# Order of grouped and memory heads, and a planner's constants, in a two-layer hybrid encoder trunk

## Chip, cores and metric

The kernel runs on one core of one Trainium2 chip. The metric is the device time of one execution in microseconds (us), as a median over several runs. Traces are of one profiled execution each, with times counted from the start of its span.

## The reference

Two layers on 1024 tokens of width 1024. Each layer normalises its input, multiplies it with one combined input projection of 3072 columns and feeds three groups of heads in parallel:

- 6 differential heads: two softmaxes each, `softmax(q1 k1) - lam * softmax(q2 k2)`, times `v`, then a per-head norm. q and k of 32 columns are turned by rotary tables.
- 6 grouped-query heads over 2 key/value heads, q and k of 64 columns with a per-head norm and a 2-D rotary.
- 4 cross-attention heads into 256 memory tokens, whose keys and values are projected from `mem`.

Cut to what matters:

```python
proj = rms_norm(x, pre_norm[l]) @ w_in[l]
oa = (softmax(q1 @ k1.T * s1) - lam * softmax(q2 @ k2.T * s1)) @ v     # 6 heads, then a norm
ob = softmax(gq @ gk.T * s2) @ gv                                      # 6 heads, 2 kv heads
om = softmax(mq @ mk.T * s2) @ mv                                      # 4 heads, 256 keys
y = concat(oa * silu(dgate), ob * silu(ggate), om * silu(mgate)) @ w_out[l]
x = x + rms_norm(y, post_norm[l])
```

All of it is float32 to the outside.

## The kernel before

**Precision by parts.** Each float32 factor of a projection is split into a high and a low part; a product is three products (high by high, high by low, low by high). Scores are made in float32 with the parts stacked along the rows of the contraction. The exponentials, 1024 columns per unit, are split into two float16 tiles `eh` (a copy on ScalarE or VectorE, lines 902 and 903) and `el` (the difference, on POOL or VectorE, lines 905 and 904).

**Items.** Attention is cut into items, each of which has three steps. *Load*: `fetch_stream` walks a list of items in order, waits for the item's `needs`, and issues its q (and k) rows from scratch in HBM through SyncE's queue. *Maxima*: `max_stream` walks the same list; TensorE makes scores in 512-column products (line 1071 for differential items, 1283 and 1284 for grouped heads, 1338 and 1339 for memory heads), VectorE takes their row maxima (line 942), and `nm_rows` turns these into two more contraction rows and stores them next to q by DMA (lines 914 to 924). *Units*: `stream` makes the scores again with the maxima subtracted inside the product (lines 1081, 1295 and 1296, 1349 and 1350), ScalarE takes the exponential (line 898), and every second unit (for memory heads every unit) `pv_part` multiplies with the values (lines 531 to 533) and ScalarE stores the result (line 994). There are 12 differential items d0 to d11 of 8 units, 6 grouped items g0 to g5 of 8 units, and 4 memory items m0 to m3 of 2 units. The grouped and memory items make one list, in the order of `GS_ORDER` (line 73). At its end `fin_g` scales a head with its gate on VectorE (lines 1200 to 1204).

**Buffers between items.** A grouped head's q rows lie in `a0`, `b0` or `a1`, `b1`, by its number's parity, so its load waits for `free` of the grouped head two before it. All memory heads have the one pair `ma`, `mb`, so a memory head's load waits for `free` of the memory head before. `free` fires when an item's last unit has been made. These tiles take slots of the ring `big`, which come free as the last projection chunk (`gg0`) finishes its 8 token tiles: `b0` and `mb` come before `b1`.

**Stages of a layer.** First the projections that the first heads need, then the differential items with the other nine projection chunks beside them (line 520), then grouped and memory items, with the splitting of the output weights and the finishing of the heads beside them, then the output projection (line 1448). When the list's last maxima have been issued, the first output tile (`z0`) is begun in the freed single banks of PSUM.

**What sets the order.** Every engine runs its instructions in the order in which they were written. That order comes from `Plan`, a small event model which runs while the kernel is built: each piece of work names an engine, a duration and a priority, and the instruction is written when the model starts it. Its durations are in `PE`, `ACT`, `DVE` and `POOL` (lines 328 to 339), e.g. `DVE_FIX` (line 75) plus columns at 960 per us for VectorE. `LAT` is the delay until another engine may go on. `SLACK` (line 81) is added after transfers. Where a step may run on two engines, the model takes the one with less queued. `DU` (line 69) is the least distance of two units' starts in the model, counted from the first unit of the stream, for differential items and for the grouped and memory list.

**PSUM.** Two tiles of two banks and four of one bank are handed out by `Banks` in the order of priority. `KINDS` (line 83) has for each kind its priority (lower goes first), how many it may hold at once, and its size in banks: `mx` are the products for maxima, `st` the projection chunks beside attention, `tr` transposes, `pv` products with the values, `zh` the first output tile. All of these are single banks.

```python
        def stream(items, kind, t0, du):
...
                for u in range(it.n_units):
                    yield "until", t_start + nu * du
                    nu += 1
                    slot = yield take_ps("un")
```

Of the kernel before, what the change touches and what calls it, by code (L numbers as in the profile page):

```python
# [65 lines left out]
LO_BIAS = (6, 1)  # L66
NAT, SQ, GS = 3, 1, 1
ALT0, ALT1, ALTM = (), (), ()
DU = (3.0, 0.0)
MXP = (0, -0.5)  # L70
SV_PRIO = -1
UNP, PVP, STP, POST, FIN = 0, 0.2, 0.5, -1, 2
GS_ORDER = ('g0', 'm0', 'g1', 'm1', 'g2', 'm2', 'g3', 'm3', 'g4', 'g5')
LAT = {"pe": 0.231, "act": 0.176, "dve": 0.165, "pool": 0.121, "hwdge": 0.65, "dma": 0.95}
DVE_FIX = 0.15
PV_N = 2
X_GATE, XT, AHEAD = 5, 5, 2
DMA_RATE = 300.0

CLOCK_WINDOW, CLOCK_LOW, CLOCK_HIGH = 3.41, 0.33, 0.85  # L80
SLACK = 0.8

KINDS = {'un': (0.5, 2, 2), 'z': (1, 2, 2), 's0': (2, 2, 1), 's1': (0, 2, 1), 'st': (1, 4, 1), 'pv': (1, 1, 1), 'tr': (-1, 2, 1), 'mx': (2, 4, 1), 'zh': (3, 2, 1)}


def raw(t):
    return t.bitcast(F32)
# [200 lines left out]
def trunk(ctx, tc, t_in, t_out):  # L288
    nc = tc.nc
    act, dve, pool, pe = nc.scalar, nc.vector, nc.gpsimd, nc.tensor  # L290
# [13 lines left out]
    banks = Banks({2: [psp.tile([P, D], F32, name=f"pp{i}") for i in range(2)],  # L304
                   1: [psp.tile([P, 512], F32, name=f"ps{i}") for i in range(4)]}, KINDS)
    R = {"rt": Ring(RT_BUFS), "wt": Ring(W_SLOTS), "big": Ring(16)}
# [9 lines left out]
    def use(eng, dur, fn, prio=0, lat=None, port=False):  # L316
        return "use", eng, dur, fn, prio, lat, port

    def wait(ev):
        return "wait", ev  # L320
# [8 lines left out]
        return use("pe", ncols / 2210.0, fn, prio, lat)  # L329

    def ACT(n, fn, prio=0, src="s"):
        return use("act", (0.2 if src == "s" else 0.17) + n / 1200.0, fn, prio)

    def DVE(n, fn, prio=0, ops=1, fast=False, port=False):

        return use("dve", DVE_FIX * ops + n / (1900.0 if fast else 960.0), fn, prio, None, port)

# [11 lines left out]
    def dmas(lst, prio=0):  # L349
        ev = Event(len(lst))  # L350
        for o, i, kb in lst:
            pl.spawn(dma(o, i, kb, prio), ev)
        return ev
# [43 lines left out]
    def split_w(rt, p2=None, name=None):  # L397
        if p2 == "big":
            wi = yield take("big")
            t = new_big()  # L400
            hi, lo = (t[:, h * 512:(h + 1) * 512].rearrange("p (a n) -> p a n", a=2) for h in range(2))
        elif p2 is None:
            wi = yield take("wt")
            hi = wp.tile([P, 2, NC], F32R, name="wt")
            lo = wp.tile([P, 2, NC], F32R, name="wt")
        else:
            wi = None
            hi = p2.tile([P, 2, NC], F32R, name=name + "h")
            lo = p2.tile([P, 2, NC], F32R, name=name + "l")
        yield ACT(512, lambda: act.activation(hi, rt, AF.Copy))  # L410
        yield either((DVE(512, lambda: dve.tensor_sub(out=lo, in0=rt, in1=raw(hi)), port=True), W_BIAS[0]),
                     (POOL(512, lambda: pool.tensor_sub(out=lo, in0=rt, in1=raw(hi))), W_BIAS[1]))  # L412
        return hi, lo, wi
# [52 lines left out]
    def split_T(src, hi, lo, halves=(0, 1), prio=0):  # L466

        done = Event(len(halves))

        def half(h):  # L470
            slot = yield take_ps("tr")
            ps = slot[3]

            def f():
                for j in range(4):
                    pe.transpose(out=ps[:, j * P:(j + 1) * P], in_=src(4 * h + j), identity=ident)  # L476

            yield PE(1024, f, prio)
            v = ps[:, 0:512].rearrange("p (b t) -> p b t", t=P)
            yield ACT(512, lambda: act.activation(hi[:, 4 * h:4 * h + 4, :], v, AF.Copy), prio, "p")  # L480
            yield DVE(512, lambda: dve.tensor_sub(out=lo[:, 4 * h:4 * h + 4, :], in0=v,
                                                  in1=raw(hi)[:, 4 * h:4 * h + 4, :]), prio)
            free_ps(slot)

        for h in halves:
            pl.spawn(half(h), done)
        yield wait(done)

    def norm_T(xt, gbc, hn, hi, lo, ev=None, alt=False, prev=None):
        ss = small.tile([P, 1], F32, name="ss")  # L490
        yield ACT(1024, lambda: act.activation(hi.rearrange("p a b -> p (a b)"), xt, AF.Square, accum_out=ss))
        box = []
        yield from rstd_of(ss, 1, 1.0 / D, box, -2)
        if ev is not None:
            yield wait(ev)
            gbc = gbc[0]
        if prev is not None:
            yield wait(prev)
        if alt:
            yield ACT(1024, lambda: act.activation(hn, xt, AF.Copy, scale=box[0][:, 0:1]))  # L500
            yield POOL(1024, lambda: pool.tensor_mul(out=hn, in0=hn, in1=gbc))
        else:
            yield DVE(1024, lambda: dve.scalar_tensor_tensor(out=hn, in0=xt, scalar=box[0][:, 0:1], in1=gbc,
                                                             op0=ALU.mult, op1=ALU.mult), port=ev is None)
        yield from split_T(lambda b: hn[:, b * P:(b + 1) * P], hi, lo, prio=0 if ev is None else -2)
# [33 lines left out]
    def make_layer(l):  # L539
# [370 lines left out]
        def nm_rows(mx, n2, scale, dst, ready):  # L910
# [17 lines left out]
            yield wait(dmas([(dst(j).rearrange("p (a b) -> p a b", b=P), raw(x), 4) for j, x in enumerate((nh, nl))]))  # L928
            yield "until", pl.t + SLACK
            ready.fire(pl)  # L930
# [24 lines left out]
        def fetched(it, ev):  # L955
            for key in it.keys:
                yield wait(gm[key + "_ev"])
            yield wait(ev)
            yield "until", pl.t + SLACK
            it.loaded.fire(pl)  # L960
# [37 lines left out]
        def stream(items, kind, t0, du):  # L998

            prev = None  # L1000
            nu = 0
            t_start = None
            for it in items:
                yield wait(it.ready)
                if t_start is None:
                    t_start = pl.t
                pl.spawn(it.fin())
                boxes, evs = [], []
# [4 lines that stand above are left out]
                    ps = slot[3]  # L1013
                    k = yield take("e32")
                    e32 = Q["at"].tile([P, 1024], F32, name="e32", bufs=E32_BUFS)
                    ncols, mm = it.unit_mm(u)
                    yield PE(ncols, lambda: mm(ps), UNP)
                    box, ev = [], Event()
                    pl.spawn(exp_part(ps, slot, it.scale, kind, box, ev, (e32, k)))
                    boxes.append(box)  # L1020
                    evs.append(ev)
                    if len(boxes) == it.per_pv:
                        d = Event()
                        pl.spawn(pv_part(it, u, boxes, evs, prev, d))
                        prev = d
                        boxes, evs = [], []
                it.free.fire(pl)
# [360 lines left out]
        def wo_setup():  # L1388
# [10 lines left out]
            v = yt[:, 0:768].rearrange("p (t c) -> p t c", t=2)  # L1399
            yield "until", pl.t + 4 * SLACK  # L1400
            yield wait(dmas([(v, y_scr[:, 0:2, 0:384], 384)]))
            yield "until", pl.t + 4 * SLACK
            for t in range(2):
# [259 lines left out]
        def main(nxt):  # L1663
# [22 lines left out]
            for i in range(4):  # L1686
                m_it.append(mk_m(i, m_it[i - 1] if i else None))
            gs = [(g_it if c[0] == "g" else m_it)[int(c[1])] for c in GS_ORDER]

# [5 lines left out]
            def d_stream():  # L1695
                yield wait(vfull["dv0"])
                yield from stream(ds, 0, 0, DU[0])
                d_units.fire(pl)
# [33 lines left out]
            def g_stream():  # L1732
                pl.spawn(fetch_stream(gs))
                pl.spawn(g_max())
                yield wait(d_units)
                yield from stream(gs, 1, 0, DU[1])
                for it in gs:
# [161 lines left out]
```

## Time and profile before

| | us |
|---|---|
| median of 3 runs | 1521.71 |
| lowest and highest of them | 1515.41, 1523.19 |
| the profiled execution | 1515.87 |
| its span, first to last instruction | 1514.1 |
| TensorE (PE) busy | 1469.9 |
| VectorE (DVE) busy | 1012.3 |
| POOL busy | 909.2 |
| ScalarE (ACT) busy | 893.3 |

A stretch's busy time of an engine is the union of its instructions in it; matmuls overlap each other, so a busy TensorE is not one at its peak. A wait is put down to what came last. The chain of waits is followed back from the last instruction of the span, at each step to what released it or to the instruction before it on its engine. PEld is the loading of weights, which runs beside PE. Layers are counted from 0.

### The profile page before, as it was taken

Reading aid. Unit: us, or ns where it says so; the run is one execution under the profiler, and the core shown is the slowest. Engines: PE = TensorE matmul, PEld = TensorE weight load, DVE = VectorE, ACT = ScalarE, POOL = GpSimd, SP = SyncE. Lnnn points to the kernel's source line nnn. Section 1 sums busy time; section 2 is a strip of 40 time slices with the busy share of each in tenths; the row PEclk is TensorE's granted clock in tenths of the full one; section 3 lists DMA queues with packets and bytes.
Section 4 is the critical chain, followed back from the end, with each engine's and each line's share of the span. In section 5 each row is a group of like instructions: output and inputs, shape, how many; then the busy total and the mean of one; then the engine's idle time right before and its main releaser. Section 6 shows DMA issues by size and latency. Waiting matters only on the chain.

```text
span 1514.1 us, 39223 instructions
## 1 busy us (share of the span) xinstructions
PE 1469.9 (97%) x15920; PEld 1362.8 (90%) x15920; DVE 1012.3 (67%) x1887; ACT 893.3 (59%) x1429; POOL 909.2 (60%) x653
## 2 busy tenths in 40 slices
PE   8999999999999999999999999999999999999997
PEld 7999989999999988888899989999999998788886
DVE  6738686777773897825466486776777649876233
ACT  5333747776677587663333346677667757686511
POOL 4233848889777586661132358579888757685400
PEclk9999999999999999999999999999999999999999
DMA  6544313233223644116164524223341256322232
GB/s 220 158 121 130 86 59 107 81 109 106 78 65 93 187 120 105 49 50 214 70 213 129 141 70 117 70 63 101 111 113 58 64 136 195 94 68 72 98 136 98
DMA packets 166658, 164.75 MB, mean 109 GB/s; under 512 B 14924, under 2 KB 140588, under 8 KB 166477
## 3 DMA queue, kind: packets, MB, share of 16 engines
q1 hardware_dynamic: 166477, 162.25, 36.7%
q8 instruction: 125, 2.05, 0.5%
q14 instruction: 56, 0.46, 0.1%
HBM read 111.74 MB, written 50.09 MB: 107 GB/s over the span
## 4 chain that ended last, share of the span: by engine, by line
PE 84%; DVE 5%; issue 3%; POOL 3%; DMA 2%; ACT 1%; SPq 1%; POOLq 0%; DVEq 0%; ACTq 0%
PE ps L520 35%; PE pp L1448 10%; PE pp L1081 6%; PE ps L1071 6%; PE ps L531 4%; PE ps L533 4%; PE ps L532 4%; PE ps L1283 3%; PE ps L1284 2%; PE pp L1295 2%; PE pp L1296 2%; POOL el L905 2%; PE ps L476 2%; DVE mx L942 1%; PE ps L707 1%
## 5 line engine op out<-in xcount | busy, mean ns | idle before, releaser
L905 POOL TENSOR_TENSOR el<-e,eh 128x1024 f16<-128x1024 f32 x254 | 562.6, 2229 | 167.3 <-ACT eh L902 160.1
L520 PE MATMUL ps<-wt,big 128*128 128x256 f32 x4608 | 642.1, 286 | 12.6 <-DVE sl L716 3.4
L520 PEld LDWEIGHTS ps<-wt,big 128*128 128x128 f32 x4608 | 605.0, 191 | 32.7 <-DVE sl L716 3.9
L942 DVE TENSOR_REDUCE mx<-ps 128x1 f32<-128x512 f32 (+1 forms) x608 | 404.0, 684 | 118.2 <-PE ps L1071 79.4
L898 ACT ACTIVATE e<-pp 128x1024 f32<-128x1024 f32 x304 | 309.2, 1023 | 99.9 <-PE pp L1081 53.8
L902 ACT ACTIVATE eh<-e 128x1024 f16<-128x1024 f32 x264 | 277.6, 1058 | 2.9
L531 PEld LDWEIGHTS <-eh 128*128 128x128 f16 x2144 | 194.4, 96 | 13.6 <-issue 9.0
L533 PEld LDWEIGHTS <-el 128*128 128x128 f16 x2144 | 196.1, 99 | 4.8 <-POOL el L905 4.2
L412 POOL TENSOR_TENSOR wt<-rt,wt 128x512 fp32r<-128x512 f32 x83 | 123.2, 1496 | 126.0 <-ACT wt L410 112.2
L532 PEld LDWEIGHTS <-eh 128*128 128x128 f16 x2144 | 196.2, 97 | 0.9 <-issue 0.8
L1071 PE MATMUL ps<-sdk,sdq 96*128 96x512 f32 x384 | 158.7, 413 | 0.8 <-DVE gs L736 0.8
L454 POOL TENSOR_SCALAR u<-ss 128x1 f32<-128x1 f32 (+3 forms) x95 | 24.2, 254 | 224.6 <-DVE ss L1589 96.1
L531 PE MATMUL ps<-vd,eh 128*128 128x65 f16 x1536 | 150.5, 193 | 0.0
L532 PE MATMUL ps<-vd,eh 128*128 128x64 f16 x1536 | 149.6, 194 | 0.0
L533 PE MATMUL ps<-vd,el 128*128 128x65 f16 x1536 | 149.1, 192 | 0.0
L1081 PE MATMUL pp<-sdq,sdk 98*128 98x256 f32 x768 | 124.9, 285 | 0.2 <-DMA sdq<-nl 0.2
L1081 PEld LDWEIGHTS pp<-sdq,sdk 98*128 98x128 f32 x768 | 113.1, 189 | 5.7 <-issue 0.6
L994 ACT ACTIVATE o<-ps 128x130 f32<-128x130 f32 (+1 forms) x160 | 46.1, 288 | 92.0 <-PE ps L533 91.4
L1295 PE MATMUL pp<-big 128*128 128x256 f32 x384 | 99.2, 290 | 0.0
L1296 PE MATMUL pp<-big 67*128 67x256 f32 x384 | 97.7, 286 | 1.3 <-DMA big<-nl 1.2
L410 ACT ACTIVATE wt<-rt 128x512 fp32r<-128x512 f32 x124 | 75.1, 630 | 18.8 <-DMA rt<-in_w_in 7.1
L455 POOL TENSOR_TENSOR r<-u,mhalf 128x1 f32<-128x1 f32 (+3 forms) x95 | 80.7, 850 | 7.9
(244 smaller groups left out, 2621.9 us busy)
## 6 DMA issues: line engine op xcount, KB each, us to landing
rt<-in_w_in SPq DMA_DIRECT2D x96, 128.0 KB
rt<-in_w_in SPq DMA_DIRECT2D x44, 256.0 KB
gt<-g_scr SPq DMA_DIRECT2D x32, 256.0 KB
rt<-in_w_out SPq DMA_DIRECT2D x32, 256.0 KB
sdq<-s_dqa SPq DMA_DIRECT2D x48, 128.0 KB
sdk<-s_dka SPq DMA_DIRECT2D x48, 128.0 KB
big<-s_gqa SPq DMA_DIRECT2D x24, 256.0 KB
big<-s_gqb SPq DMA_DIRECT2D x24, 256.0 KB
```

The lines of the kernel that those rows point to most:

```text
L520: pe.matmul(ps, lhsT=x[:, kt, :], rhs=y[:, a, :], start=(kt == 0 and n == 0), stop=(kt == KT - 1 and n == 2))
L531: pe.matmul(o[:, 0:65], lhsT=eh, rhs=v[:, kt, 0:65], start=(kt == 0), stop=False, skip_group_check=True)
L532: pe.matmul(o[:, 0:64], lhsT=eh, rhs=v[:, kt, 66:130], start=False, stop=False, skip_group_check=True)
L533: pe.matmul(o[:, 0:65], lhsT=el, rhs=v[:, kt, 0:65], start=False, stop=(kt == n - 1), skip_group_check=True)
L898: yield ACT(1024, lambda: act.activation(e, ps, AF.Exp, scale=scale), 0, "p")
L902: yield either((ACT(1024, lambda: act.activation(eh, e, AF.Copy)), 0.0), (DVE(1024, lambda: dve.tensor_copy(out=eh, in_=e), 0, fast=True, ...
L905: (POOL(1024, lambda: pool.tensor_sub(out=el, in0=e, in1=eh)), 0.0))
L942: yield DVE(512, lambda: dve.tensor_reduce(out=out_ap, in_=src, axis=AX.X, op=ALU.max), MXP[0])
L1071: yield (512, lambda ps, n=n: pe.matmul(ps, lhsT=q()[0:96, i * P:(i + 1) * P], rhs=k()[0:96, n * 512:(n + 1) * 512], start=True, stop=True ...
L1081: pe.matmul(ps[:, a * 256:(a + 1) * 256], lhsT=k()[0:98, kt * P:(kt + 1) * P], rhs=q()[0:98, j * 256:(j + 1) * 256], start=True, stop=True)
L1295: pe.matmul(o, lhsT=ka()[:, ks], rhs=a()[:, qs], start=True, stop=False)
L1448: pe.matmul(z, lhsT=x[:, k, :], rhs=y, start=(k == KT_ORDER[0] and n == 0), stop=(k == KT_ORDER[-1] and n == 2))
```

## The change

The list of grouped and memory items becomes g0, g1, m0, g2, m1, g3, m2, g4, m3, g5: from g2 on a memory head stands one grouped head later than before. The kind `mx` may hold three single banks instead of four. The model's figures change: `DVE_FIX` from 0.15 to 0.117 us, the fixed part of a ScalarE instruction from 0.2 to 0.201 us with its source in SBUF and from 0.17 to 0.138 us with it in PSUM, `SLACK` from 0.8 to 0.7 us, and the step of differential units from 3.0 to 2.85 us. No instruction's form or size changes; orders, and choices between two engines, can.

```diff
--- before.py
+++ after.py
@@ -66,21 +66,21 @@
 LO_BIAS = (6, 1)
 NAT, SQ, GS = 3, 1, 1
 ALT0, ALT1, ALTM = (), (), ()
-DU = (3.0, 0.0)
+DU = (2.85, 0.0)
 MXP = (0, -0.5)
 SV_PRIO = -1
 UNP, PVP, STP, POST, FIN = 0, 0.2, 0.5, -1, 2
-GS_ORDER = ('g0', 'm0', 'g1', 'm1', 'g2', 'm2', 'g3', 'm3', 'g4', 'g5')
+GS_ORDER = ('g0', 'g1', 'm0', 'g2', 'm1', 'g3', 'm2', 'g4', 'm3', 'g5')
 LAT = {"pe": 0.231, "act": 0.176, "dve": 0.165, "pool": 0.121, "hwdge": 0.65, "dma": 0.95}
-DVE_FIX = 0.15
+DVE_FIX = 0.117
 PV_N = 2
 X_GATE, XT, AHEAD = 5, 5, 2
 DMA_RATE = 300.0
 
 CLOCK_WINDOW, CLOCK_LOW, CLOCK_HIGH = 3.41, 0.33, 0.85
-SLACK = 0.8
-
-KINDS = {'un': (0.5, 2, 2), 'z': (1, 2, 2), 's0': (2, 2, 1), 's1': (0, 2, 1), 'st': (1, 4, 1), 'pv': (1, 1, 1), 'tr': (-1, 2, 1), 'mx': (2, 4, 1), 'zh': (3, 2, 1)}
+SLACK = 0.7
+
+KINDS = {'un': (0.5, 2, 2), 'z': (1, 2, 2), 's0': (2, 2, 1), 's1': (0, 2, 1), 'st': (1, 4, 1), 'pv': (1, 1, 1), 'tr': (-1, 2, 1), 'mx': (2, 3, 1), 'zh': (3, 2, 1)}
 
 
 def raw(t):
@@ -329,7 +329,7 @@
         return use("pe", ncols / 2210.0, fn, prio, lat)
 
     def ACT(n, fn, prio=0, src="s"):
-        return use("act", (0.2 if src == "s" else 0.17) + n / 1200.0, fn, prio)
+        return use("act", (0.201 if src == "s" else 0.138) + n / 1200.0, fn, prio)
 
     def DVE(n, fn, prio=0, ops=1, fast=False, port=False):
```

## Rows read from the trace of the kernel before

**Rows 1.** The page: busy time of each engine, and the chain by engine.

```profile
PE 1469.9 (97%) x15920; PEld 1362.8 (90%) x15920; DVE 1012.3 (67%) x1887; ACT 893.3 (59%) x1429; POOL 909.2 (60%) x653
...
PE 84%; DVE 5%; issue 3%; POOL 3%; DMA 2%; ACT 1%; SPq 1%; POOLq 0%; DVEq 0%; ACTq 0%
```

**Rows 2.** Busy by stretch: length, PE, PEld, DVE, ACT, POOL; clock, DMA share, GB/s.

```profile
142.90:511.00 368.10, 362.34 (x4501) 347.33 (x4501) 258.81 (x540) 248.16 (x391) 280.22 (x198) 1.00 0.34 95
888.20:1257.10 368.90, 363.10 (x4503) 347.90 (x4504) 260.16 (x539) 248.45 (x392) 280.21 (x198) 1.00 0.34 94
533.10:572.80 39.70, 35.04 (x483) 30.84 (x481) 36.02 (x50) 28.20 (x39) 29.38 (x14) 1.00 0.53 129
1278.60:1318.00 39.40, 35.06 (x484) 30.58 (x481) 35.82 (x50) 28.68 (x41) 29.52 (x14) 1.00 0.53 132
572.80:596.70 23.90, 23.29 (x298) 20.41 (x296) 17.45 (x28) 19.86 (x24) 17.97 (x9) 1.00 0.15 44
596.70:631.20 34.50, 34.28 (x434) 28.97 (x431) 30.33 (x44) 22.40 (x30) 21.30 (x10) 1.00 0.33 79
650.70:674.70 24.00, 22.90 (x378) 21.16 (x378) 5.39 (x4) 17.41 (x23) 18.06 (x9) 1.00 0.06 18
```

**Rows 3.** Chain that ended last, transfers in the grouped part: start, us.

```profile
534.03 6.16 DMA big<-s_mqa
564.93 7.02 DMA big<-s_gqa
...
1309.88 7.22 DMA big<-s_gqa
```

**Rows 4.** Busy by stretch, line 1295 alone: PE and PEld of g0, g1.

```profile
511.50:528.00 16.50, 7.58 (x30) 5.58 (x31) 1.00 0.49 151
533.00:556.60 23.60, 7.75 (x31) 5.88 (x31) 1.00 0.43 103
```

**Rows 5.** Busy by stretch, line 1349 alone: PE and PEld of m0, m1, m2.

```profile
528.90:532.40 3.50, 1.40 (x4) 0.76 (x4) 1.00 0.92 298
557.40:561.50 4.10, 1.27 (x4) 0.66 (x4) 1.00 0.23 64
592.30:594.20 1.90, 1.57 (x4) 0.77 (x4) 1.00 0.00 0
```

**Rows 6.** Busy by stretch: maxima of m2 (line 1338); g2, g3, g5 (line 1283).

```profile
566.50:571.00 4.50, 2.21 (x8) 1.52 (x8) 1.00 1.03 215
...
544.80:562.70 17.90, 6.55 (x16) 3.03 (x16) 1.00 0.06 16
571.20:589.90 18.70, 7.03 (x16) 2.99 (x16) 1.00 0.24 72
624.40:638.80 14.40, 7.35 (x17) 2.89 (x16) 1.00 0.16 46
```

**Rows 7.** Timeline of SyncE's queue, 455 to 512 us: start, us.

```profile
496.94 1.73 SPq L346 DMA_DIRECT2D big<-s_gqa  x3
```

**Rows 8.** Busy by stretch, columns as in rows 2.

```profile
568.00:570.00 2.00, 1.25 (x10) 1.25 (x11) 0.58 (x1) 0.00 (x0) 0.00 (x0) 1.00 1.03 228
1316.00:1318.00 2.00, 0.85 (x4) 0.68 (x4) 0.47 (x2) 0.00 (x0) 0.00 (x0) 1.00 0.94 309
1318.00:1320.00 2.00, 2.00 (x10) 1.80 (x9) 1.04 (x3) 0.13 (x1) 0.00 (x0) 0.59 0.03 12
1320.00:1322.00 2.00, 2.00 (x11) 1.88 (x10) 0.80 (x2) 1.96 (x2) 0.00 (x0) 0.56 0.00 0
```

**Rows 9.** Timelines of ScalarE and of VectorE, 545 to 556 us.

```profile
546.89 1.92 ACT L898 ACTIVATE e<-pp 128x1024 f32<-128x1024 f32 x2
...
550.57 4.40 DVE L942 TENSOR_REDUCE mx<-ps 128x1 f32<-128x512 f32 x7
```

**Rows 10.** Busy by stretch, line 1081 alone: differential units, four products each.

```profile
142.80:189.90 47.10, 10.44 (x64) 9.16 (x64) 1.00 0.32 88
212.20:483.50 271.30, 52.03 (x320) 47.26 (x320) 1.00 0.31 88
```

## Prediction

> **What bounds the kernel now.** I read the page's busy line and its chain first [rows 1]: TensorE is busy 97% of the span and carries 84% of the chain that ended last. The change takes no product away, so only two things can move the end: time in which TensorE has nothing to do, and time at the lower clock. Next I read the busy time by stretch [rows 2]. "Idle" below is a stretch's length less TensorE's busy time. In the differential stretch of each layer it is 368.10 - 362.34 = 5.76 us and 368.90 - 363.10 = 5.80 us. In the grouped and memory part of layer 0 it is 39.70 - 35.04 = 4.66 us between the first units of g1 and g2, then 0.61 us to g3's first unit, 0.22 us to g4's, and 1.10 us in g5's stretch, which runs on to the output projection. Layer 1 repeats the large one: 39.40 - 35.06 = 4.34 us. In that stretch VectorE is busy 36.02 of 39.70 us, so it is nearly a second bound there; in the next it has 17.45 of 23.90.
>
> The chain of waits names what ends the large idle time [rows 3]: transfers of 6.16, 7.02 and 7.22 us of q rows for the next heads. Those loads wait in `fetch_stream` for `prev.free`, the end of the units of the memory head before, since all memory heads share `ma` and `mb`. Behind them stand the maxima, in the order of the list: m1's, then g2's.
>
> **The order of heads.** I follow it as one recurrence. Call c the time from the end of a memory head's units to the first unit of the grouped head that is loaded behind the next memory head. The units of g0 run from 511.5 to 528.0 and g1's from 533.0 to 556.6 [rows 4]; m0's end at 532.4, m1's at 561.5, m2's at 594.2 [rows 5]. With the starts in rows 2, c is 572.8 - 532.4 = 40.4, 596.7 - 561.5 = 35.2 and 631.2 - 594.2 = 37.0 us. Its parts: transfers, 7.0 us [rows 3]; a memory head's maxima, 4.5 us; a grouped head's maxima, 14.4 us where little else competes, 17.9 and 18.7 us elsewhere; from there to the first unit 596.7 - 589.9 = 6.8 or 572.8 - 562.7 = 10.1 us [rows 2, 6]. The shortest sum is 7.0 + 4.5 + 14.4 + 6.8 = 32.7 us.
>
> With the new list, g0 does not change. g1's maxima no longer stand behind m0's. They can't start at once either: g1's q rows are issued at 496.94 whatever the order, since its tiles come free only then [rows 7]. A 6 to 7 us transfer has them in by about 503 to 504, some 4 us before they start now, so its units can start at 533.0 - 4 = 529, about where g0's end; I take 528.5. They take 23.6 us as before [rows 4], m0's two units about 4.9 (4.1 of rows 5 and the last product's tail), and m0 ends at 557.0. g2's loads now wait for g0 alone: 528.0 + 7.0 + 17.9 + 10.1 = 563.0. TensorE is without units for 563.0 - 557.0 = 6.0 us where it is now 572.8 - 561.5 = 11.3.
>
> This gain is given back in part, for m1's work is not done by then and moves behind g2. From there the old pattern runs once per pair: g3 starts c after m0's end; m2 ends 21.4 us after g3's first unit (594.2 - 572.8, the same pair of stretches now); g5 starts c after that, its maxima now standing behind m3's loads. g5's first unit is thus at 557.0 + c + 21.4 + c = 578.4 + 2c, against 650.7 now. They are equal at c = 36.15. Of the measured values I take 34.0, between the shortest sum 32.7 and the 35.2 of the middle pair: TensorE was busy through most of that middle stretch [rows 2], and in the new one a memory head's units and maxima more stand elsewhere. Then g5 starts at 646.4, 4.3 us sooner, and its 24.0 us stretch [rows 2] moves with it. The first output tile still begins after g5's maxima, at 646.4 - 6.8 = 639.6 against 638.8 [rows 6], so its cover stays. Ends: c = 32.7 gives -6.9, c = 37.0 gives +1.7, c = 40.4 gives +8.5 us per layer. Two layers: -8.6 us.
>
> **The clock in that gap.** In layer 1 TensorE is busy 0.85 of 2 us at 1316, and the granted clock then is 0.59 and 0.56 of full (1.2 GHz for most of both rows, 2.4 GHz outside); 2.00 x 0.41 + 2.00 x 0.44 = 1.7 us are lost there [rows 8]. In layer 0 the like stretch at 568 has 1.25 of 2 us and keeps 1.00. Only part of it reaches the end: I count 1.0 us gained in layer 1 when the gap halves; ends 0 and 1.7. The Trainium skill (TensorE: Matmul & The Clock Gate, Part 1: The HAM clock gate) says the throttled state is the default and recent activity is what releases it; layer 1 agrees with its 0.59, layer 0 with 1.00 shows that a gap of this size may pass, and by the rule alone every such gap would pay the price.
>
> **Three products for maxima instead of four.** A maximum takes VectorE 4.40 / 7 = 0.63 us back to back [rows 9]. TensorE makes its pair of products in about 0.41 us (6.55 / 16) [rows 6], so three banks, 1.9 us of VectorE's work, cover it: 0. If TensorE is away longer, with two units' products and the second matrix, VectorE runs dry for one bank's worth, 0.63 us; four times per head this adds 2.5 us to c, which is 5.0 us per layer. Below nothing: a bank left to projections can end some of the idle 5.8 us of the differential stretch; that end is counted with the next edit.
>
> **The planner's figures and slack.** They cost no time and change only orders: 0.033 us less per VectorE operation, 0.032 us less per ScalarE read of PSUM, 0.1 us less after a transfer. The plan had 0.15 + 512 / 960 = 0.683 us for a maximum and has 0.650 now, against 0.63; for an exponential 0.17 + 1024 / 1200 = 1.023 and now 0.991, against 1.92 / 2 = 0.96 [rows 9]. So plan and chip come closer without meeting. What mistimed orders can cost is bounded by the idle time of the differential stretches, 5.76 + 5.80 = 11.6 us: all gone, or as much again. I take an eighth, -1.5 us, since part of each error stays and an idle time may move as well as go.
>
> **The step of 2.85 us.** The first 16 units come in 47.1 us, 47.1 / 16 = 2.94 from edge to edge, near the planned 3.0; the other 80 take 271.3 us, 3.39 each [rows 10]. The pace binds only the first two items, which end 15 x 0.15 = 2.25 us sooner. Nothing is won: TensorE has projections to do beside them (362.34 of 368.10 us busy [rows 2]), which must be done before the grouped heads load. I take 0; ends -2.25 us and, if POOL and ScalarE are crowded by it, +2.25 us per layer.
>
> **Sum.** -8.6 - 1.0 - 1.5 = -11.1 us against the profiled execution's 1515.87 us (span 1514.1 and 1.8 around it): 1504.8. The median of the runs shown, 1521.71, stands 5.8 us above that execution, so the forecast as a median is 1510.6, written as 1511.
>
> **Rivals.** *Slower: VectorE late for three banks.* If the pairs keep the 37.0 us of the third one and the smaller limit adds its 2.5, c is 39.5; g5 starts at 578.4 + 79.0 = 657.4, 6.7 us later per layer, 13.4 in all: 1529.3, as a median 1535. It decides from c = 36.15 upward and is measurable from about 38. For it: VectorE's 36.02 of 39.70 us in the first such stretch [rows 2]. Against: it is near 17 of 24 in the next. *No change: the gap only moves.* With c from 36 to 37, what g2 gains the later pairs give back, and the rest is noise: 1515 to 1519, as a median 1521 to 1525. For it: two of three measured values of c lie above 36.15. *The clock falls in each new gap.* The new order waits ahead of g3 and g5 as it did once ahead of g2. With c at 36.15 and both gaps of both layers paying 1.7 us, that is +6.8: 1522.7, median 1528.5. For it layer 1, against it layer 0 [rows 8]. [...] *The change doesn't do what it says:* the limit of 2.85 is such an edit already; for the whole I see no way, since the list sets the streams directly.
>
> **How the numbers follow.** Forecast 0.50, no change 0.25, slower 0.18, clock 0.07. Half a per cent, 7.6 us, is about what a measurement of this kernel can tell from no change; the runs shown already span 7.8. Faster by more than that: most of the forecast's own 0.50, whose median range runs from 1495 (c = 32.7 twice, 13.8; the clock 1.0; nearly all idle of the differential stretches) to 1518, less a tenth that falls short, and a little from the others: 0.47. Slower: most of its rival and a third of the clock's: 0.19. Same: 0.34. The range 1495 to 1530 leaves out the worst of the slower rival and a full sweep of gains.
>
> **What would show it.** Right: g1's units directly after g0's, at about 529 us; m0's between g1 and g2; a first g2 unit at 560 to 565, and g5's first unit before 650; idle under 3 us where it was 4.66; granted clock 1.00 there in layer 1. Wrong: idle of several us ahead of g3 or g5 with the chain naming q rows or maxima; g5's first unit after 652; VectorE waiting for products inside the maxima; more idle than 5.8 us in the differential stretch.

## The result, and the profile after

The changed kernel takes **1530.13 us** (median; 1528.42 to 1531.01) beside 1521.71 us before: a ratio of 1.0063 [1.0038, 1.0087], slower by 0.63%. That is 8.4 us where 11 us less were forecast, and just outside the range. The profiled execution has 1528.42 us with a span of 1526.6, 12.5 us above the span before; 4.1 us of this are the choice of executions, since the one before stands 5.8 us under its median and this one 1.7. (Three kernels below had one disturbed execution of over 2000 us, which is left out; in `all_but_order` and `warm_products` it was the profiled one, so no row of these two is used.)

The page of the changed kernel, its busy line and its chain by engine, answer to [rows 1]:

```profile
PE 1479.1 (97%) x15920; PEld 1369.0 (90%) x15920; DVE 1033.3 (68%) x1892; ACT 893.7 (59%) x1429; POOL 892.3 (58%) x648
...
PE 81%; DMA 6%; DVE 5%; POOL 3%; issue 3%; SPq 1%; ACT 1%; POOLq 0%; DVEq 0%; ACTq 0%
```

The work is the same. TensorE's share of the chain went from 84% to 81%: transfers now end last more often (DMA 6% where it was 2%). Where, the busy time by stretch says (columns as in [rows 2]; the first two lines are the differential stretches, then g1's first unit to g2's, to g3's, to g4's, to g5's, and g5's stretch; then g1 to g2 in layer 1; last the front of layer 1, from the first projection product to the first differential unit):

```profile
142.00:509.00 367.00, 364.88 (x4501) 348.48 (x4501) 265.00 (x542) 248.59 (x392) 274.39 (x195) 1.00 0.34 95
896.00:1263.70 367.70, 364.82 (x4499) 348.61 (x4500) 264.49 (x540) 248.50 (x390) 273.94 (x194) 1.00 0.34 94
526.40:569.20 42.80, 36.88 (x471) 31.68 (x471) 36.04 (x45) 25.77 (x36) 27.03 (x14) 0.91 0.42 106
569.20:591.30 22.10, 22.05 (x245) 19.47 (x244) 16.68 (x26) 17.80 (x23) 14.10 (x7) 0.94 0.16 44
591.30:628.60 37.30, 36.14 (x488) 31.47 (x487) 30.42 (x47) 25.04 (x34) 23.37 (x11) 1.00 0.44 111
628.60:652.00 23.40, 23.02 (x254) 20.14 (x253) 15.98 (x26) 19.83 (x24) 16.17 (x8) 1.00 0.15 42
652.00:677.50 25.50, 24.41 (x386) 22.38 (x384) 9.68 (x9) 19.00 (x25) 18.92 (x9) 1.00 0.20 58
1281.60:1321.20 39.60, 35.32 (x471) 30.66 (x471) 37.25 (x44) 25.75 (x36) 27.50 (x14) 0.96 0.45 113
767.30:896.00 128.70, 123.32 (x993) 119.77 (x991) 81.40 (x173) 40.60 (x86) 38.19 (x41) 1.00 0.47 140
```

The same front in the kernel before:

```profile
764.50:888.20 123.70, 122.31 (x993) 119.72 (x992) 78.44 (x171) 39.87 (x85) 35.80 (x39) 1.00 0.51 147
```

Read each line as length less busy time. The differential stretches got better (idle 2.12 and 2.88 us, where [rows 2] gave 5.76 and 5.80). The gap ahead of g2 did not close: 42.80 - 36.88 = 5.92 us, where it was 4.66. And the front of layer 1, of which the prediction does not speak, has 5.38 us of idle time where it had 1.39. Taken by the starts of the units in the two traces, the 12.5 us are: start of the kernel -0.9, differential stretches -1.7 and -1.1, grouped and memory parts (g0's first unit to the last product with the values) +5.5 and +3.9, front of layer 1 +5.1, output projections -0.2 and +1.9.

How much of the grouped parts' share is waiting and how much slower products, the whole parts show, changed kernel first (layers 0, 1), then before:

```profile
509.00:677.40 168.40, 158.48 (x2027) 139.89 (x2026) 124.19 (x170) 124.14 (x164) 116.71 (x56) 0.97 0.33 87
1263.70:1431.60 167.90, 157.24 (x2028) 139.16 (x2028) 125.81 (x170) 124.44 (x164) 117.41 (x56) 0.98 0.31 84
```

```profile
511.50:674.40 162.90, 155.22 (x2022) 136.67 (x2022) 123.22 (x168) 125.01 (x164) 119.34 (x56) 1.00 0.34 90
1257.10:1421.00 163.90, 156.53 (x2025) 137.88 (x2024) 120.54 (x168) 124.87 (x164) 119.64 (x56) 0.99 0.32 86
```

Idle time went from 7.68 to 9.92 and from 7.37 to 10.66 us, 5.5 us more; busy time rose by 3.26 and 0.71, 4.0 us, for five and three products more, at a lower mean clock.

**The gap ahead of g2.** The lines of 1295 alone (a grouped or memory unit's first product) show the end of g1's units and a hole in them:

```profile
526.40:531.50 5.10, 2.75 (x11) 2.03 (x11) 1.00 0.64 194
531.50:540.80 9.30, 0.51 (x3) 0.36 (x3) 0.66 0.53 149
540.80:551.50 10.70, 4.62 (x19) 3.63 (x19) 0.98 0.09 26
```

TensorE's timeline in the hole says what stands there:

```profile
531.73 0.28 PE L1295 MATMUL pp<-big 128*128 128x256 f32 x1
531.85 0.28 PE L1296 MATMUL pp<-big 67*128 67x256 f32 x1
534.12 0.47 PE L1283 MATMUL ps<-big 128*128 128x512 f32 x1 [1.99 <-DMA big<-s_gqa]
535.17 0.79 PE L1284 MATMUL ps<-big 65*128 65x512 f32 x1 [0.58 <-DMA big<-s_gqa]
...
541.12 0.36 PE L1295 MATMUL pp<-big 128*128 128x256 f32 x1
```

Products of line 1283 are those for g2's maxima. The plan placed the first of them among g1's units, counting on q rows that had not landed. TensorE ran them in the order written, so units of g1 stood behind it: no unit's product starts from 531.85 to 541.12. They were not waiting for ScalarE, which has no exponential to take from 534.25 to 542.42. SyncE's queue and the chain show how the rows came:

```profile
525.24 2.57 SPq L346 DMA_DIRECT2D rt<-in_w_out  x2
527.90 1.78 SPq L346 DMA_DIRECT2D big<-s_gqa  x3
```

```profile
525.18 2.28 POOL wt L412
527.48 0.33 SPq L346
...
529.10 6.03 DMA big<-s_gqa
560.30 6.82 DMA big<-s_gqa
...
768.31 4.80 DMA sub<-in_diff_subln
...
795.31 8.37 DMA s_dka<-sh
```

Two loads of W_out stand ahead of g2's rows on the queue. The row's 2.57 us are not two issues: one takes 0.33 us, and the second waits until POOL is done with its buffer (line 412) and is issued at 527.48. g0's last unit, which frees the tiles for g2's rows, starts its last product at 526.17, so this load holds the rows back by little more than 1 us; the transfer lasts to 535.1.

The chain's line at 768.31 is the same fault on another engine: in the front of layer 1 a small VectorE operation on `sub` (line 618) was put into VectorE's queue ahead of the tiles' norm, and waits there until its transfer ends at 773.1:

```profile
773.13 0.20 DVE L618 TENSOR_SCALAR sub<-sub 128x64 f32<-128x64 f32 x1 [1.42 <-DMA sub<-in_diff_subln]
```

It is not on the chain of the kernel before, though VectorE waits 1.0 us for the same transfer there. VectorE's wait is 1.42 us, so it alone does not make the front's 5.1; the chain has a longer item in that front, its last line above, a store for whose buffer ScalarE waits. What the rest of the 5.1 us is stays open.

### The profile page after: what moved, and what is told of

Its sections match the earlier page's. It is cut to its first block, busy times and chain, and to the rows that moved or that the text cites. A ratio compares the mean times of both kernels' runs of the same rounds, so it can differ in the third digit from the quotient of the medians.

```text
span 1526.6 us, 39193 instructions
## 1 busy us (share of the span) xinstructions
PE 1479.1 (97%) x15920; PEld 1369.0 (90%) x15920; DVE 1033.3 (68%) x1892; ACT 893.7 (59%) x1429; POOL 892.3 (58%) x648
## 4 chain that ended last, share of the span: by engine, by line
PE 81%; DMA 6%; DVE 5%; POOL 3%; issue 3%; SPq 1%; ACT 1%; POOLq 0%; DVEq 0%; ACTq 0%
PE ps L520 33%; PE pp L1448 9%; PE ps L1071 6%; PE pp L1081 6%; PE ps L531 4%; PE ps L532 4%; PE ps L533 4%; PE ps L1283 2%; PE ps L1284 2%; PE pp L1296 2%; PE pp L1295 2%; PE ps L476 2%; DMA big<-s_gqb 2%; SPq L346 1%; POOL el L905 1%
## 5 line engine op out<-in xcount | busy, mean ns | idle before, releaser
L1283 PE MATMUL ps<-big 128*128 128x512 f32 x192 | 83.1, 433 | 5.3 <-DMA big<-s_gqa 2.4
```

## The experiments

Ratios are to the kernel before, timed beside it on the same chip, with 95% intervals. Stage lengths below run between starts of products in the profiled execution, in us.

**The order alone.** Kernel before, with the new list:

```
-GS_ORDER = ('g0', 'm0', 'g1', 'm1', 'g2', 'm2', 'g3', 'm3', 'g4', 'g5')
+GS_ORDER = ('g0', 'g1', 'm0', 'g2', 'm1', 'g3', 'm2', 'g4', 'm3', 'g5')
```

> The kernel before with the new list of heads and nothing else. Theory (the order costs: g2's maxima stand in TensorE's queue during g1's units and wait there for rows, and the clock falls): slower by 6 to 14 us than before, with a stop of several us inside g1's units and low-clock stretches beside it. Rival (the other edits, which redraw every order, cost the time): within 4 us of before.

Measured 1548.65 us, 1.0198 [1.0179, 1.0218]: far slower than the whole change. Nearly all of it is lost in the grouped parts, 178.8 and 176.2 us where they were 162.9 and 163.9.

**All but the order.** The changed kernel with the old list.

> The changed kernel with the old list of heads. Theory (the order costs): 6 to 14 us faster than the changed kernel, so within 4 us of before or a little faster, since the differential stretch gained 2 to 5 us per layer with the new figures. Rival (the other edits cost): as slow as the changed kernel, 1526 to 1532 us.

1534.39 us, 1.0088 [1.0064, 1.0112]. The same kernel once more, for its trace:

> The changed kernel with the old list of heads once more, for its trace. As before, 8 to 15 us slower than before. If the waits ahead of maxima are its loss too: units of a grouped head stop behind a memory head's maxima that wait for rows, as in the changed kernel.

1532.41 us, 1.0084 [1.0060, 1.0108]. So the parts don't add: +2.0% and +0.9% apart, +0.6% together.

**The parts one at a time and in pairs.**

```
-DU = (3.0, 0.0)
+DU = (2.85, 0.0)
```

> The kernel before with a step of 2.85 us for differential units alone. Theory (any redraw loses): 5 to 20 us slower than before. Rival (the step binds 16 units and shortens the chain of the first two items): within 3 us, or a little faster.

1534.05 us, 1.0096 [1.0073, 1.0120]. The stretches of this kernel, differential and grouped, layer 0:

```profile
142.70:503.40 360.70, 356.59 (x4453) 340.97 (x4453) 252.93 (x532) 247.46 (x387) 269.51 (x192) 1.00 0.32 90
503.40:681.10 177.70, 166.36 (x2073) 146.97 (x2073) 133.57 (x186) 123.94 (x166) 115.97 (x55) 0.97 0.35 96
```

A limit that binds two items took 8 us out of one stage and put 15 into the next. In part products moved: the grouped part has 2073, 51 more than before, and the differential stretch fewer by about as many than in [rows 2]; TensorE's busy time fell by 362.34 - 356.59 = 5.75 us there and rose by 166.36 - 155.22 = 11.14 here, with 11.34 us of idle time where it was 7.68.

```
-... 'mx': (2, 4, 1) ...
+... 'mx': (2, 3, 1) ...
```

> The kernel before with three banks for maxima alone. Theory (VectorE's queue is covered by three): within 3 us of before. Rival (VectorE runs dry): 5 us slower or more, with more idle time of VectorE before maxima than before's 118 us.

1538.16 us, 1.0129 [1.0102, 1.0156]; grouped parts 174.7 and 171.9. VectorE's idle time before maxima is 143.8 us instead of 118.2, as the rival said; but it is 135.7 in the kernel with the step alone, which has four banks.

```
-DVE_FIX = 0.15
+DVE_FIX = 0.117
-SLACK = 0.8
+SLACK = 0.7
-    (0.2 if src == "s" else 0.17)
+    (0.201 if src == "s" else 0.138)
```

> The kernel before with the new figures and slack alone. Theory (figures nearer to the trace help the differential stretch and upset the start of layer 1's projections and TensorE's queue in the grouped part): between 2 us faster and 10 us slower than before, with the first differential unit of layer 1 3 to 5 us later than layer 0's end makes it. Rival (figures nearer to the trace are harmless): 2 to 6 us faster.

1536.09 us, 1.0107 [1.0088, 1.0126]: grouped parts 167.8 and 167.2, and the front of layer 1 at 130.4 instead of 123.7. The two pairs, order with three banks and order with figures:

> The new list and three banks for maxima, all figures as before. If the limit is what made the changed kernel bear the new list: near 1530 us, some 18 us below the list alone. If the figures did: within 5 us of the list alone (1548 us).

> The new list with the new figures and slack, four banks and the step of 3.0 us. If the figures made the changed kernel bear the new list: near 1530 us. If the limit of three did: within 5 us of the list alone (1548 us).

1.0139 [1.0095, 1.0184] and 1.0158 [1.0105, 1.0212]. Both are within 5 us of the order alone, and neither gives the change's 1.0063; no part explains the whole.

**Is it the clock?** In the changed kernel the granted clock falls in layer 0 as the last rival said (four stretches of 4 us, the third with 3.30 us busy at 0.56):

```profile
526.00:530.00 4.00, 3.51 (x64) 3.17 (x64) 3.97 (x6) 4.00 (x7) 4.00 (x3) 1.00 0.54 174
530.00:534.00 4.00, 2.13 (x18) 1.92 (x17) 4.00 (x4) 4.00 (x7) 4.00 (x2) 1.00 0.90 215
534.00:538.00 4.00, 3.30 (x43) 2.71 (x44) 2.67 (x4) 0.25 (x1) 2.24 (x2) 0.56 0.65 209
538.00:542.00 4.00, 4.00 (x25) 3.42 (x22) 2.31 (x5) 2.78 (x5) 2.49 (x3) 0.59 0.07 11
```

In its grouped parts 10.2 and 6.8 us lie at the lower level (1.2 GHz), against 0 and 3.4 before. To see what that costs, eight needless products were put ahead of the first maxima product of g2, g3, m1 and m2, with their planned cost left out so that the order of all else stays as it was; their results are overwritten.

```
+for _ in range(8):
+    pe.matmul(ps, lhsT=k[:, 0:P], rhs=k[:, 512:1024], start=True, stop=True)
 mm(ps)
```

On the changed kernel:

> The changed kernel with every instruction in its order, and 8 needless products of 512 columns put ahead of the first product for maxima of g2, m1, g3 and m2 in each layer (about 1.9 us each at full clock, 64 in all). If the low clock after these waits is a large part of the loss: the stretches at half clock at 534, 568, 1316 and 1350 us vanish and the kernel gets faster by 3 to 8 us in spite of the added work. Rival (the waits themselves are the loss, the clock runs low only where TensorE waits anyway): same or slower by up to 5 us.

1525.30 us, 1.0037 [1.0023, 1.0051]. That is 4.8 us faster by the medians, with a granted clock of 0.997 to 0.999 over whole executions where the changed kernel has 0.990 to 0.993; but the interval still overlaps the change's own, so this alone settled nothing. On the order alone, where the grouped parts have 27.3 and 13.7 us at the lower level:

> The kernel with the new list alone, its instructions in the same order, and 8 needless products of 512 columns ahead of the first maxima product of g2, m1, g3 and m2 (64 in all, 15 us at full clock). Theory (the low clock is most of that kernel's loss: in its trace the grouped parts run 27 and 14 us at half clock, which is some 20 us lost): 8 to 20 us faster than the list alone, with half-clock stretches gone or much shorter. Rival (the waits are the loss, the clock follows them at no cost): same or up to 10 us slower.

1549.87 us, 1.0183 [1.0136, 1.0229]. First `order_only`, its grouped part of layer 0 and 10 us in it, then `order_warm`:

```profile
512.50:691.30 178.80, 164.64 (x2026) 147.53 (x2025) 107.38 (x168) 126.09 (x163) 120.38 (x58) 0.92 0.31 82
606.00:616.00 10.00, 9.91 (x50) 9.02 (x50) 5.99 (x13) 6.35 (x8) 4.37 (x3) 0.74 0.21 54
```

```profile
512.50:691.30 178.80, 164.96 (x2063) 147.29 (x2062) 107.82 (x168) 125.80 (x163) 120.78 (x58) 0.97 0.31 82
606.00:616.00 10.00, 9.32 (x59) 7.99 (x58) 8.52 (x17) 7.48 (x9) 5.16 (x3) 1.00 0.26 73
```

Time at the lower level fell from 41.0 to 17.0 us over both layers; at half the speed, 24.0 us less is worth 12.0 us of products. The grouped part kept its length. That looks as if the clock cost nothing, but the run does not say so: the fillers take time themselves. One group of eight in `order_warm`:

```profile
602.30 2.09 PE L936 MATMUL ps<-big 128*128 128x512 f32 x8
```

The eight groups have 2.00 to 3.31 us, 19.3 in all; that is what they cost if TensorE had other work ready each time, more than the 12.0 at stake. By the medians gain and cost cancel to about 2 us, with an interval of 7 us either way, and how much of each there was stays open. What the clock can have cost the changed kernel is bounded in another way: half of 17.0 us at the lower level less half of 3.4 is 6.8 us, and the busy time of its grouped parts rose by 4.0, of the 9.4 us that they lost. The other 5.5 us are idle time. (A price of the clock without a new order stands below, under the edits without a meaning.)

**Is it the wait in TensorE's queue?** Here the plan counts q rows as landed 2.5 us later than it did, for grouped and memory heads alone; nothing is taken out of the kernel.

```
-            yield "until", pl.t + SLACK
+            yield "until", pl.t + SLACK + (2.5 if it.keys else 0.0)
```

On the changed kernel, on the order alone and on the kernel before:

> The changed kernel with the planner told that rows of grouped and memory heads land 2.5 us later, so that their maxima are written later into TensorE's queue. Theory (units stand behind maxima that wait for rows): g1's units no longer stop for 10 us, and the kernel gets faster by 3 to 10 us. Rival (the rows come late for the next head whatever stands ahead of the maxima): same, or slower by 1 to 5 us.

> The kernel with the new list alone, its planner told that rows of grouped and memory heads land 2.5 us later. Theory (maxima that wait for rows stand in TensorE's queue ahead of units that are ready): 15 to 30 us faster than the list alone, near before. Rival (the new list makes the rows themselves late for the next head): gains under 5 us.

> The kernel before, its planner told that rows of grouped and memory heads land 2.5 us later. Theory (maxima that wait for rows stand ahead of ready units in the kernel before too: 4.7 us idle between g1 and g2): 3 to 8 us faster than before. Rival (there the rows are late for the next head itself): within 2 us.

1518.60 us, 0.9997 [0.9988, 1.0007]; 1537.83 us, 1.0100 [1.0076, 1.0125]; 1525.97 us, 1.0042 [1.0026, 1.0058]. By the medians the first two are 11.5 and 10.8 us faster than the kernels that they mend, by the ratios, each to before on its own chip, about 10 and 15; the third is slower, which neither its theory nor its rival said. In `late_maxima` the stretch from g1's first unit to g2's is

```profile
528.10:564.40 36.30, 32.98 (x469) 28.85 (x468) 34.78 (x47) 26.76 (x38) 27.06 (x12) 1.00 0.50 127
```

6.5 us shorter than in the changed kernel, idle 3.32 us instead of 5.92, the clock at 1.00, and g2 begins at 564.4, close to the 563.0 of the prediction. g5's first unit is at 646.4, the forecast to the tenth, where the changed kernel has 652.0. That is luck: m0 ends at 553.0 (557.0 forecast), the first c is 31.9 us (34.0), m2 ends 26.3 us after g3's first unit (21.4), and the second c is 35.1 (34.0); the errors cancel. (At the end of the part 2.7 of the 4.3 us forecast are left, and the front of layer 1, at 128.3, takes more than them back.) The gain fits the wait as a cause. But this edit too makes the planner draw the orders anew, from the first grouped maxima on, and the kernel before has no such hole and became slower: so part of any of the three differences is the new order as such. The next runs measure that.

**Edits without a meaning.** One figure of the plan is changed by less than half a per cent; nothing in the kernel's work, buffers or heads changes.

```
-SLACK = 0.8
+SLACK = 0.803
```

> The kernel before with a slack of 0.803 us in the planner instead of 0.8. The edit means nothing; it redraws the orders. Theory (the orders of before are a good draw, and any redraw loses): 5 to 20 us slower than before. Rival (what the edits mean costs the time): within 3 us of before.

```
-DVE_FIX = 0.15
+DVE_FIX = 0.1502
```

> The kernel before with a fixed part of 0.1502 us instead of 0.15 for VectorE in the planner. Theory (any redraw loses): 5 to 20 us slower than before. Rival (the edits' meaning): within 3 us.

```
-DMA_RATE = 300.0
+DMA_RATE = 300.5
```

> The kernel before with 300.5 instead of 300 KB per us for transfers in the planner. Theory (any redraw loses): 5 to 20 us slower than before. Rival (the edits' meaning): within 3 us.

1537.16 us, 1.0116 [1.0097, 1.0135]; 1530.60 us, 1.0072 [1.0051, 1.0093]; 1540.43 us, 1.0139 [1.0107, 1.0171]. **Edits that mean nothing cost 11 to 21 us**, as much as most parts of the change. On the changed kernel, `DVE_FIX` 0.1172 for 0.117:

> The changed kernel with a fixed part of 0.1172 us instead of 0.117 for VectorE in the planner. Theory (redraws scatter by 10 us and more, whatever they mean): anything from 5 us faster to 15 us slower than the changed kernel, more than 3 us off it. Rival (the edits' meaning sets the time): within 3 us of the changed kernel.

1532.49 us, 1.0075 [1.0047, 1.0103], no different from the change: here the rival's outcome came, and a redrawn order cost nothing that can be told. How far chance goes, one kernel shows with itself. The grouped parts of layers 0 and 1 of `null_slack`, the same code with two orders:

```profile
513.10:677.60 164.50, 156.10 (x2023) 137.99 (x2022) 122.62 (x168) 125.22 (x164) 118.47 (x56) 0.99 0.34 89
1258.30:1442.10 183.80, 165.02 (x2060) 145.73 (x2059) 140.93 (x182) 123.06 (x164) 112.75 (x57) 0.97 0.33 88
```

and its chain in the second names one VectorE operation behind which TensorE's work stood:

```profile
1306.44 8.46 DVE elm L904
```

In all these traces operations of this line take 1.2 to 3.2 us, but for this one and one of 6.06 in `null_rate`; in both cases POOL runs three or four operations beside it without a pause. What makes them so long no run shows.

**The same order, executed again.** These edits do not redraw everything. Read line by line, each engine's instructions in `null_slack` come in the order of before up to 969 us, in `null_rate` up to 804 (times in the trace of before). So their layer 0 is the order of before, executed again, and yet its grouped part takes 164.5 and 170.9 us instead of 162.9. In `null_rate` the granted clock falls in the gap ahead of g2, where it stayed at 1.00 in the kernel before (the whole part, then the gap):

```profile
512.40:683.20 170.80, 162.04 (x2024) 143.21 (x2023) 120.14 (x168) 125.28 (x164) 118.49 (x56) 0.95 0.33 86
...
568.00:570.00 2.00, 0.71 (x6) 0.72 (x7) 0.07 (x2) 0.00 (x0) 0.00 (x0) 1.00 1.02 234
570.00:572.00 2.00, 2.00 (x13) 2.00 (x12) 1.96 (x4) 0.28 (x1) 0.00 (x0) 0.60 1.04 224
```

TensorE is busy 0.71 of 2 us before the fall; in the kernel before it had 1.25 [rows 8]. With 0, 3.4 and 17.1 us at the lower level (1.2 GHz) the same order takes 162.9, 164.5 and 170.9 us: about half of that time is lost, 6.82 of the last 8.0 us as longer busy time of TensorE.

The stages of all the profiled orders beside one another, one execution each (fillers left out):

| kernel | differential, layers 0, 1 | grouped, layers 0, 1 | front of layer 1 |
|---|---|---|---|
| before | 368.7, 368.8 | 162.9, 163.9 | 123.7 |
| changed | 367.0, 367.7 | 168.4, 167.8 | 128.8 |
| changed, `DVE_FIX` 0.1172 | 367.2, 368.7 | 169.2, 169.2 | 130.9 |
| all but order | 367.5, 367.4 | 173.8, 168.6 | 130.0 |
| order alone | 369.9, 371.0 | 178.8, 176.2 | 123.4 |
| three banks alone | 370.2, 369.6 | 174.7, 171.9 | 123.5 |
| figures alone | 371.1, 371.1 | 167.8, 167.2 | 130.4 |
| step alone | 360.7, 359.9 | 177.7, 178.0 | 123.4 |
| order, three banks | 370.9, 371.5 | 178.5, 171.2 | 123.4 |
| order, figures | 369.0, 370.2 | 181.5, 170.6 | 127.2 |
| `SLACK` 0.803 | 370.2, 366.9 | 164.5, 183.8 | 123.8 |
| `DVE_FIX` 0.1502 | 364.9, 364.0 | 177.0, 170.2 | 123.9 |
| `DMA_RATE` 300.5 | 368.6, 368.7 | 170.9, 182.1 | 127.5 |
| late_maxima | 366.1, 367.1 | 163.4, 165.4 | 128.3 |
| order_late | 370.2, 370.1 | 166.9, 168.5 | 123.3 |
| before_late | 379.4, 372.2 | 167.8, 166.5 | 123.3 |
| mixed_front | 366.9, 367.1 | 163.7, 165.6 | 125.4 |

Each of the sixteen has a longer grouped part than this one trace of before in both layers, and fourteen of the sixteen are slower than it by more than their interval. But single rows scatter by the execution: by 8 us for `null_rate` above, and 379.4 in `before_late`, whose order is that of before up to 482 us, comes from an execution nearly 12 us over that kernel's median. So the medians carry the argument, and a stage's difference of a few us in one trace does not.

**The later maxima with the old figures in the front.** The front of layer 1 is near 123.5 us in nearly all orders with the old figures and 127 to 131 in all with the new ones. So `late_maxima` was run with the old figures for VectorE and ScalarE from the end of layer 0 to the first differential unit of layer 1.

```
-            yield wait(L.go)
+            yield wait(L.go); NEAR[0] = l == 0
...
-                yield wait(vfull["dv0"])
+                yield wait(vfull["dv0"]); NEAR[0] = True
```

(`DVE` and `ACT` take the old figures while `NEAR[0]` is false.)

> The changed kernel with maxima 2.5 us later in the plan, whose planner has the old figures for VectorE and ScalarE from the end of layer 0 to the first differential unit of layer 1. Layer 0 is as in that kernel. Theory (the front's 5 us come from the figures, the rest is a draw): the front of layer 1 in 123 to 125 us instead of 128.3; in all 1510 to 1516 us if the grouped part of layer 1 is drawn as well as there (165 us), up to 1530 if not. Rival (the front is a draw too): its length anywhere from 123 to 131 us.

1516.38 us, 0.9982 [0.9968, 0.9996]. The front shrank from 128.3 to 125.4 us; `sub`'s transfer stays on the chain. It is the only version that beats both kernels, the one before by 0.2%; as one of sixteen orders, it may owe that to the draw.

## Why the prediction was wrong

By stage, two things failed. The term for the order of heads, -8.6 us, came as +9.4 in the grouped parts; which steps of its sum were off stands below. And the front of layer 1, for which the prediction has no term, took 5.1 us more. The differential stretches, to which it gave -1.5, came as -2.8.

**The failed step** under both, as far as the runs show, is this one: the figures and the slack "cost no time and change only orders", with their worth bounded "by the idle time of the differential stretches" and taken as an eighth of it, -1.5 us. A changed order is not cheap here. Three meaningless edits of the planner's figures cost 11 to 21 us, all in stages outside that bound: most of it in the grouped parts, part of it (`DMA_RATE`) in the front of layer 1. The idle of the differential stretches was the smallest part of what an order can do, and the prediction bounded the term by it because it was where the trace of before still showed idle time. The same holds for each other edit: the list, the three banks and the step all make the planner draw the orders anew from the point where they first bind. The rival that was missing is "any new order loses about a per cent", and it belonged to the likeliest cases. Why the order of before is so good is open; that it was picked among many such orders would explain it, but that is an inference.

**The order of heads**, forecast at -4.3 us per layer, came as +5.5 and +3.9. In layer 0 its early steps look right: g1 begins directly after g0, at 526.5 (528.5 forecast), m0 ends at 557.2 (557.0), and the first c is 591.3 - 557.2 = 34.1 (34.0). But the part began 2.5 us sooner than before (509.0 against 511.5), and g1's units, with the hole in them, took 25.1 us instead of 23.6. Counted from the part's start, m0 ends 2.7 us late. m0 to m2 by their line (1349 alone):

```profile
553.30:557.20 3.90, 1.58 (x4) 0.58 (x4) 1.00 0.02 4
587.70:591.20 3.50, 1.72 (x4) 0.76 (x4) 1.00 0.03 7
611.60:616.20 4.60, 1.59 (x4) 0.61 (x4) 1.00 0.50 142
```

Three more steps fail. g2, forecast at 563.0, comes at 569.2: its rows land at 535.1, as forecast (528.0 + 7.0), but its maxima, 534.1 to 559.2, take 25 us instead of 17.9. m2 ends 616.2 - 591.3 = 24.9 us after g3's first unit, not 21.4; and the second c is 652.0 - 616.2 = 35.8. So g5 begins at 652.0: 0.2 + 0.1 + 3.5 + 1.8 = 5.6 us after the forecast's 646.4, and 8.1 after it by the part's own start; g5's own stretch adds 1.5. Of the 3.5, 2.7 are m2's own two units: 4.6 us where they took 1.9 in the kernel before [rows 5], from which the 21.4 was copied, though m0 and m1 took 3.5 and 4.1 there. Layer 1 shows the same (c of 33.4 and 35.4 us, 28.4 between g3's first unit and m2's end). g2's delay is not in the sum, since m0's end does not hang on it. Of the prediction's signs, g1 right after g0 and m0 ahead of g2 came true, and so did "wrong: g5's first unit after 652", by a hair.

**The clock.** The sum's gain of 1.0 did not come; the clock falls in four places of the two grouped parts, as the rival said. The Trainium skill (TensorE: Matmul & The Clock Gate, Part 1: The HAM clock gate) has the throttled state as the default, released by recent activity; the trace agrees with the 0.56 after the idle time at 532 to 534 and four falls in the two grouped parts. That neither makes a fall certain in every gap nor lets a gap of this size pass, as the prediction's two readings had it: the gap ahead of g2 in layer 0, in the order of before, kept 1.00 in one trace and fell to 0.60 in another. The rival's price of +6.8 us is what the 17.0 us at the lower level give as a bound, and 4.0 us of longer busy time were found. So this rival was right in kind and is a part of the result, with a chance of 0.07. It follows the waits in part: in `late_maxima`, without the wait ahead of g2, the grouped part of layer 0 has no fall, but that of layer 1 has 6.8 us at the lower level as in the changed kernel.

**Three banks** were put at 0 with +5.0 us per layer as the end. Alone they cost 1.3%, more than that end, yet no more than a meaningless edit does: their own cost can't be read off one run. The prediction's 0.41 us for a pair of products is one product's recorded time (line 1283 alone has 6.55 / 16); with line 1284 the pair comes every 0.47 us in the trace of before, still under VectorE's 0.63. VectorE's 36.04 of 42.80 us between g1 and g2 does not speak for the rival in which it is late; there it waits for products behind q rows. **The step** was put at 0 within 2.25 us per layer; alone it moved -8 and +15 us in layer 0, far outside that bound and as much as other new orders do.

**What holds and what stays open.** Shown: edits without a meaning cost the kernel before 11 to 21 us, so no part of the change can be priced by one run; the work queued behind an unlanded transfer (on TensorE ahead of g2, on VectorE in the front of layer 1) is in the trace, and a later planned landing took the first away and 10 to 11.5 us with it. Argued only: how much of these is that wait, how much the clock and how much the luck of a new order, since no edit of the plan changes one place alone; and that the waits, not the draw, made the changed kernel slower than before. Not tried: the kernel before with its instruction order written down and only one head moved by hand, which would price the list by itself.

## What to carry to other kernels

Where a planner or scheduler draws the order of the instructions, first run two or three edits that mean nothing; their spread (here +0.7% to +1.4% on the kernel before, +0.1% on the changed one) is what one run of any real edit must exceed before its meaning may be read from it, and a tuned kernel is to be expected at the good end of that spread. Compare stages of two traces only where the same order, executed twice, agrees better than the difference. In a trace, look less at how long an idle time is than at which ready work stands in an in-order queue behind an instruction whose transfer has not landed. To price one suspect, hold the instruction order and change one thing; and a filler that is put in to keep a clock up has a time of its own, to be measured before the run is read.

## What the runs showed of the hardware

On SyncE's queue one load of W_out takes 0.33 us to issue and one of q rows 0.51 to 0.59; a load that waits for its buffer (to 527.48 us here, for POOL) holds up those behind it. The transfers of rows on the chain landed 6.0 and 6.8 us after their start, near those of [rows 3], though the 16 DMA engines were at 0.54 and 0.90 of their time from 526 to 534 us and near 1.0 in the gaps of [rows 8].

The same instructions in the same order ran the grouped part of layer 0 in 162.9, 164.5 and 170.9 us, with 0, 3.4 and 17.1 us at the lower clock. A VectorE operation that takes 1.2 to 3.2 us elsewhere took 8.46 and 6.06 in two places, each beside three or four POOL operations without a pause; why is open.
